# Where split weight chunks and MLP activations lie in SBUF: 224 bytes for stationary chunks, 32 bytes for the activations

## Chip, cores and metric

The kernel runs on one core of one Trainium2 chip. The metric is the device time of one execution in microseconds (us); lower is better. The time before is 747.07 us, the median of three runs.

## What is computed

A causal decoder trunk of two layers over 256 tokens of width 1024, in float32. Each layer is a mixer and a squared-ReLU MLP, with a LayerNorm after each:

```python
for layer in range(DEPTH):                      # DEPTH = 2
    h = rwkv_moba_mixer(x, ...) if layer % 2 == 0 else dilated_mixer(x, ...)
    x = layer_norm(ALPHA * x + h, ln1_g[layer], ln1_b[layer])
    mlp = square(relu(x @ w1[layer])) @ w2[layer]          # 1024 -> 4096 -> 1024
    x = layer_norm(ALPHA * x + mlp, ln2_g[layer], ln2_b[layer])
```

Layer 0's mixer is RWKV-7 time mixing (8 heads of 64) beside a block attention (4 heads of 128), with one input and one output projection. Layer 1's mixer is a dilated window attention: 8 heads of 128, each with one key, one value and three query projections.

## The kernel before

**Weights come as 211 chunks.** The host cuts every weight matrix into chunks of 128 partitions by 1024 floats (4096 bytes a partition, 512 KB each) in the order in which they are used. `Stream` (L51 on) loads them through SyncE's DMA queue into a ring of `raw` tiles. Chunks from number 17 on (`UNSPLIT`) are split: ScalarE copies `raw` to `hi` in the type float32r (L89), and VectorE, for twelve chunks GpSimd, writes the remainder `lo = raw - hi` (L91). `add_pairs` (L62) allocates the places for `hi` and `lo`: four pairs at the start, four more once layer 0's mixer has freed its memory. `place` (L93) hands them out in turn.

**A product is three float32r matmuls.** With both operands split, hi·hi, hi·lo and lo·hi are added in PSUM. Activations are split too: `xh`, `xl` (the layer's input, transposed), `yh`, `yl` (a mixer's output) and `hh`, `hl` (the MLP's hidden values). Each TensorE matmul has one operand that is loaded into the array beforehand, the *stationary* one (128 columns, so 512 bytes of each partition), and one that is *streamed* through it (256 or 512 columns, so 1024 or 2048 bytes of each partition). Every matmul here has its own weight load. There are two helpers:

- `wstat` (L207, matmuls at L218) keeps a weight chunk stationary and streams `xh` or `xl`, 256 tokens at a time. It is used for the projections into heads (L0's r, gate and block attention heads, all of layer 1's q and k) and for three quarters of the MLPs' first matrix. 90 chunks go this way after number 17, with 24 matmuls each: 2160.
- `xstat` (L221, matmuls at L223, L224, L225) keeps 128 tokens of an activation stationary and streams half a weight chunk, 512 columns. It is used for the output projections, value projections, the first quarter of the MLPs' first matrix (with `xh`, `xl` stationary) and the whole second matrix (`hh`, `hl` stationary). In the very last MLP, token half 1 has its right half in two streams of 256 columns (`acc_banks`, L295), so that 192 of its matmuls are 256 wide.

**Order of an MLP** (`mlp`, L354): a first quarter of the hidden values token by token (`by_token`, L338), then groups of eight `wstat` chunks (`up`) and of eight `xstat` chunks (`down`, 96 matmuls), and the last group in `tail` (L302), which ends each token half with its LayerNorm.

**Addresses.** A tile pool puts tiles one after another. The tile `x` (L1047), the LayerNorm tiles and, above them, the MLP tiles `r`, `s`, `hh`, `hl` lie in pools that are opened after the second four pairs. Nothing else about the layout is fixed by hand.

Of the kernel before, what the change touches and what calls it, by code (L numbers as in the profile page):

```python
# [11 lines left out]
F32 = mybir.dt.float32  # L12
F32R = mybir.dt.float32r
# [6 lines left out]
P = 128  # L20
T = 256
D = 1024
# [16 lines left out]

UNSPLIT = 17  # L40
ON_POOL = (34, 36, 37, 38, 39, 42, 100, 150, 151, 161, 164, 169)
NW1, NW2, NR, NR2 = 4, 4, 4, 2
NS4, NS2 = 13, 6
RIGHT = "right"
# [6 lines left out]
class Stream:  # L51
# [9 lines left out]

    def add_pairs(self, pool, n):  # L62

        new = [(pool.tile([P, D], F32R, name=f"hi{len(self.pairs) + i}"), pool.tile([P, D], F32R, name=f"lo{len(self.pairs) + i}"))
               for i in range(n)]
        self.pairs = new + self.pairs[self.pos:] + self.pairs[:self.pos]
        self.pos = 0
# [23 lines left out]
        eng.tensor_tensor(lo[:, cols], r[:, cols], hi[:, cols].bitcast(F32), ALU.subtract)  # L91

    def place(self, i):  # L93
        self.hl[i] = self.pairs[self.pos]
        self.pos = (self.pos + 1) % len(self.pairs)
        return self.hl[i]

# [22 lines left out]
def trunk(ctx: ExitStack, tc: tile.TileContext, w_all, x_nat, x_t, par_in, lora_in, gup2_in, ln_in,  # L120
# [80 lines left out]
    st.load(1 + NR)  # L201
    st.on_pool = set(ON_POOL)

# [32 lines left out]
    def bload(pool, i, nm):  # L236
        t = pool.tile([P, D], F32, tag=nm, name=f"{nm}{i}")
        nc.sync.dma_start(out=t, in_=ln_in[i:i + 1, :].partition_broadcast(P))
        return t
# [805 lines left out]
    cur["look"] = NW1 + NW2 - 2  # L1045
    lnp = ctx.enter_context(tc.tile_pool(name="lnp", bufs=1, reuse_waits="tile"))
    x = lnp.tile([P, 2, D], F32, name="x")  # L1047
    nc.sync.dma_start(out=x, in_=x_nat)
    g = bload(lnp, 0, "g")
    b = bload(lnp, 1, "b")  # L1050
# [258 lines left out]
```

## Time and profile before

| | |
|---|---|
| runs shown | 747.22, 743.59, 747.07 us (median 747.07) |
| the profiled execution | 743.96 us, its span 741.9 us |
| mean granted TensorE clock | 0.981 |
| PE (matmuls) busy | 711.9 us, 96% of the span |
| PEld (weight loads) busy | 632.2 us, 85% |
| DVE, ACT, POOL busy | 476.4, 333.9, 156.4 us |
| DMA | 122.61 MB, 165 GB/s in the mean |

PE is TensorE's matmuls and PEld its weight loads, which run beside matmuls; DVE is VectorE, ACT ScalarE, POOL GpSimd. Matmuls are pipelined: the duration that a row gives for one (0.28 or 0.39 us here) is longer than the distance from its start to the next one's start, and it is this distance, the *pace*, that a row of matmuls takes. Line numbers are those of the kernel before.

### The profile page before, as it was taken

How to read it: one execution, taken by the hardware profiler on the slowest of the kernel's cores; microseconds unless marked ns; L12 is line 12 of the kernel's file. 1: busy time of each engine (PE TensorE's matmuls, PEld its weight loads, DVE VectorE, ACT ScalarE, POOL GpSimd, SP SyncE). 2: the span in 40 equal slices, each digit the busy share in tenths (PEclk: the TensorE clock that was granted, in tenths of full speed). 3: DMA queues.
4: the chain of work that ended last, by engine and by line, in shares of the span. 5: the costliest groups of instructions: out<-in, count | busy, mean ns of one | idle time of the engine just before them, and what ended most of it. 6: DMA issues, size and time to landing. Idle time of an engine off the chain costs nothing. (4 is left out here: it accounts for less than half of the span.)

```text
span 741.9 us, 11557 instructions
## 1 busy us (share of the span) xinstructions
PE 711.9 (96%) x4572; PEld 632.2 (85%) x4572; DVE 476.4 (64%) x733; ACT 333.9 (45%) x485; POOL 156.4 (21%) x115
## 2 busy tenths in 40 slices
PE   9999998997999999999999899989999999999995
PEld 7867887986889889889879899988878898998985
DVE  3838973679686446546598668874497654464645
ACT  4712445253365335445255456545436453453420
POOL 3000041036100000000116767884131110000001
PEclk9999997998999999999999999999999999999998
DMA  8455461046584656555088433452537566555401
GB/s 305 142 176 181 137 190 44 30 175 252 169 284 151 200 188 197 173 199 180 20 297 302 143 114 115 149 168 83 169 125 245 168 198 189 190 192 172 142 1 58
DMA packets 40566, 122.61 MB, mean 165 GB/s; under 512 B 8128, under 2 KB 10816, under 8 KB 40384
## 3 DMA queue, kind: packets, MB, share of 16 engines
q1 hardware_dynamic: 37856, 119.94, 48.7%
q10 hardware_dynamic: 2656, 1.93, 0.9%
q8 instruction: 36, 0.59, 0.3%
q14 instruction: 18, 0.15, 0.1%
HBM read 119.49 MB, written 2.36 MB: 164 GB/s over the span
## 5 line engine op out<-in xcount | busy, mean ns | idle before, releaser
L91 DVE TENSOR_TENSOR lo<-raw,hi 128x1024 fp32r<-128x1024 f32 x182 | 236.4, 1303 | 145.4 <-ACT hi L89 143.7
L89 ACT CAST hi<-raw 128x1024 fp32r<-128x1024 f32 x194 | 202.1, 1048 | 207.1 <-PE bank L224 100.7
L218 PE MATMUL bank<-xh,hi 128*128 128x256 f32 x720 | 180.3, 288 | 0.0
L218 PE MATMUL bank<-xl,hi 128*128 128x256 f32 x720 | 178.2, 285 | 0.0
L218 PEld LDWEIGHTS bank<-xh,hi 128*128 128x128 f32 x720 | 138.8, 193 | 1.5 <-issue 0.7
L218 PEld LDWEIGHTS bank<-xl,hi 128*128 128x128 f32 x720 | 139.0, 193 | 0.5
L224 PE MATMUL bank<-hi,hl 128*128 128x512 f32 (+1 forms) x288 | 106.7, 371 | 1.9 <-DVE hl L234 1.9
L225 PE MATMUL bank<-lo,hh 128*128 128x512 f32 (+1 forms) x288 | 106.4, 370 | 0.0
L223 PE MATMUL bank<-hi,hh 128*128 128x512 f32 (+1 forms) x288 | 105.5, 370 | 0.3 <-ACT hh L233 0.3
L218 PE MATMUL bank<-xh,lo 128*128 128x256 f32 x720 | 101.8, 283 | 0.0
L218 PEld LDWEIGHTS bank<-xh,lo 128*128 128x128 f32 x720 | 93.0, 192 | 0.0
L266 POOL TENSOR_TENSOR rs<-rs,mhalf 128x1 f32<-128x1 f32 x8 | 7.7, 963 | 327.5 <-DVE rs L265 327.5
L854 POOL TENSOR_TENSOR qk<-qk,ropec 32x512 f32<-32x512 f32 x20 | 49.8, 2490 | 76.5 <-DVE sw L852 76.5
L224 PEld LDWEIGHTS bank<-hi,hl 128*128 128x128 f32 x288 | 54.0, 188 | 12.5 <-DVE hl L234 2.5
L223 PEld LDWEIGHTS bank<-hi,hh 128*128 128x128 f32 x288 | 53.9, 188 | 10.6 <-ACT hh L233 0.5
L225 PEld LDWEIGHTS bank<-lo,hh 128*128 128x128 f32 x288 | 54.0, 188 | 9.9
L210 PE MATMUL bank<-xst,raw 128*128 128x256 f32 x208 | 46.7, 384 | 0.5 <-DMA xst<-in_x_t_dram 0.5
L210 PEld LDWEIGHTS bank<-xst,raw 128*128 128x128 f32 x208 | 39.9, 193 | 7.4 <-DMA xst<-in_x_t_dram 1.2
L91 POOL TENSOR_TENSOR lo<-raw,hi 128x1024 fp32r<-128x1024 f32 x12 | 30.3, 2532 | 56.8 <-ACT hi L89 56.8
L225 PE MATMUL bank<-lo,xh 128*128 128x512 f32 x96 | 37.7, 393 | 0.6 <-DVE lo L91 0.6
L223 PE MATMUL bank<-hi,xh 128*128 128x512 f32 x96 | 38.0, 396 | 0.0
L224 PE MATMUL bank<-hi,xl 128*128 128x512 f32 x96 | 37.5, 391 | 0.1
(236 smaller groups left out, 896.0 us busy)
## 6 DMA issues: line engine op xcount, KB each, us to landing
raw<-in_w_all_dram SPq DMA_DIRECT2D x210, 512.0 KB, 3.5
g<-in_ln_dram SPq DMA_DIRECT2D x4, 512.0 KB, 5.1
b<-in_ln_dram SPq DMA_DIRECT2D x4, 512.0 KB, 6.7
dA<-abT ACTq DMA_DIRECT2D x2, 512.0 KB, 3.6
x<-in_x_nat_dram SPq DMA_DIRECT2D x1, 1024.0 KB, 4.9
dmask<-in_dmask_dram SPq DMA_DIRECT2D x1, 576.0 KB, 5.9
xst<-in_x_t_dram ACTq DMA_DIRECT2D x2, 256.0 KB, 5.6
xst<-in_x_t_dram SPq DMA_DIRECT2D x2, 256.0 KB, 5.7
```

What stands on the lines that cost most here:

```text
L89: self.nc.scalar.copy(hi[:, cols], r[:, cols])
L91: eng.tensor_tensor(lo[:, cols], r[:, cols], hi[:, cols].bitcast(F32), ALU.subtract)
L210: nc.tensor.matmul(ps, hl[:, k * P:(k + 1) * P], xraw(k), start=k == 0, stop=k == KT - 1)
L218: nc.tensor.matmul(ps, w[:, k * P:(k + 1) * P], a[:, k, :], start=n == 0, stop=n == 3 * KT - 1)
L223: nc.tensor.matmul(acc, ah, hi[:, cols], start=first, stop=False)
L224: nc.tensor.matmul(acc, al, hi[:, cols], start=False, stop=False)
L225: nc.tensor.matmul(acc, ah, lo[:, cols], start=False, stop=last)
L266: nc.gpsimd.tensor_tensor(rs, rs, mhalf, ALU.pow)
L854: nc.gpsimd.tensor_tensor(qk[0:32, :], qk[0:32, :], rc, MUL)
```

## The change

```diff
+STATIONARY = [1] * 9 + [0] * 4 + [1] * 14 + [0] * 8
+_MLP = [0] * 8 + [1] * 8 + [0] * 16 + ([1] * 8 + [0] * 8) * 2
+STATIONARY += _MLP + [0] * 4 + [1] * 32 + [0] * 12 + _MLP
+LINE, STAT_AT = 64, 56
@@ add_pairs
-        new = [(pool.tile([P, D], F32R, name=f"hi{len(self.pairs) + i}"), pool.tile([P, D], F32R, name=f"lo{len(self.pairs) + i}"))
+        new = [(pool.tile([P, D + LINE], F32R, name=f"hi{len(self.pairs) + i}"), pool.tile([P, D + LINE], F32R, name=f"lo{len(self.pairs) + i}"))
@@ place
-        self.hl[i] = self.pairs[self.pos]
+        o = STAT_AT if STATIONARY[i] else 0
+        self.hl[i] = tuple(t[:, o:o + D] for t in self.pairs[self.pos])
@@ trunk
     x = lnp.tile([P, 2, D], F32, name="x")
+    lnp.tile([P, 8], F32, name="pad")
```

`STATIONARY` tells of each chunk whether `wstat` will use it. A place for `hi` or `lo` becomes 1088 floats, 4352 bytes = 17 times 256. A chunk for `wstat` is written 56 floats, 224 bytes, into its place; a chunk for `xstat` at the place's beginning. An unused tile of 32 bytes behind `x` moves all that lies above it: the LayerNorm tiles, `vd`, and the MLP's `hh` and `hl`. The built program has the same instructions as before, in the same order and with the same waits, on every engine; only addresses differ. Of the operands of float32r matmuls they are, as the remainder of a tile's (or chunk's) first byte in the partition after division by 256:

| operand | before | after |
|---|---|---|
| `hi`, `lo` of a chunk that `wstat` keeps stationary | 128 | 96 |
| `hi`, `lo` of a chunk that `xstat` streams | 128 | 128 |
| `xh`, `xl`, `yh`, `yl` | 128 | 128 |
| `hh`, `hl` | 96 | 128 |

Slices inside these tiles start at multiples of 512 bytes, so that the remainders hold for them too. Call *distance* the stationary operand's remainder less the streamed one's. Before, it is 0 for `wstat`, 0 for `xstat` with `x` and `y`, and -32 for `xstat` with the MLP's `hh` and `hl`. After, it is -32 for `wstat` and 0 for every `xstat`. Of the other tiles, the LayerNorms' `g`, `b`, `u` go from 128 to 160.

## Rows read from the trace of the kernel before

**Rows 1.** The page: the span, and each engine's busy time, share and instructions.

```profile
span 741.9 us, 11557 instructions
...
PE 711.9 (96%) x4572; PEld 632.2 (85%) x4572; DVE 476.4 (64%) x733; ACT 333.9 (45%) x485; POOL 156.4 (21%) x115
```

**Rows 2.** The page: the chain that ended last, shares by engine, then by line.

```profile
PE 36%; DVE 6%; POOL 3%; issue 3%; ACT 1%; POOLq 0%; DVEq 0%
PE bank L218 17%; PE bank L225 6%; PE bank L224 6%; PE bank L223 5%; DVE lo L91 2%; POOL qk L854 2%; PE bank L1113 1%; POOL qk L856 1%; PE bank L1111 1%; DVE u L253 1%; ACT hi L89 1%; DVE sw L852 1%; DVE st L254 0%; ACT e L1119 0%; DVE x L279 0%
```

**Rows 3.** Groups by line and shape, PE: count, busy us, mean ns, idle before.

```profile
L218 PE MATMUL bank<-xh,hi 128*128 128x256 f32 x720 | 180.3, 288 | 0.0
L218 PE MATMUL bank<-xl,hi 128*128 128x256 f32 x720 | 178.2, 285 | 0.0
L218 PE MATMUL bank<-xh,lo 128*128 128x256 f32 x720 | 101.8, 283 | 0.0
...
L223 PE MATMUL bank<-hi,hh 128*128 128x512 f32 x224 | 87.9, 396 | 0.3 <-ACT hh L233 0.3
...
L223 PE MATMUL bank<-hi,hh 128*128 128x256 f32 x64 | 17.8, 280 | 0.0
```

**Rows 4.** Timeline in layer 1: a weight load starts with the matmul before its own.

```profile
300.83 0.19 PEld L218 LDWEIGHTS bank<-xh,hi 128*128 128x128 f32 x1
300.95 0.28 PE L218 MATMUL bank<-xh,hi 128*128 128x256 f32 x1
300.95 0.19 PEld L218 LDWEIGHTS bank<-xl,hi 128*128 128x128 f32 x1
```

**Rows 5.** The chain in order of time: start us, us, engine and line, count.

```profile
386.39 19.91 PE bank L218 x166
...
406.30 0.67 PE bank L1111 x6
...
583.39 17.27 PE bank L218 x144
```

**Rows 6.** Timeline, PE: first row of a `down` group and first row behind it.

```profile
303.83 0.39 PE L223 MATMUL bank<-hi,hh 128*128 128x512 f32 x1
...
326.23 0.28 PE L218 MATMUL bank<-xh,hi 128*128 128x256 f32 x1
```

**Rows 7.** Timeline, PE: first and last of a 512-wide run with `xh` stationary.

```profile
372.53 0.39 PE L223 MATMUL bank<-hi,xh 128*128 128x512 f32 x1
...
376.84 0.39 PE L224 MATMUL bank<-hi,xl 128*128 128x512 f32 x1
```

**Rows 8.** Timeline, PE: first and last of the 256-wide run at the end.

```profile
728.25 0.28 PE L223 MATMUL bank<-hi,hh 128*128 128x256 f32 x1
...
733.73 0.28 PE L225 MATMUL bank<-lo,hh 128*128 128x256 f32 x1
```

**Rows 9.** Two `up` groups by windows: PE, PEld, DVE, ACT, POOL busy; clock, DMA share, GB/s.

```profile
643.40:665.70 22.30, 22.30 (x188) 22.30 (x187) 13.69 (x14) 11.93 (x15) 0.00 (x0) 1.00 0.56 190
688.80:711.10 22.30, 22.30 (x189) 22.30 (x188) 13.69 (x14) 11.93 (x15) 0.00 (x0) 1.00 0.29 96
```

**Rows 10.** Waits of PE: us in total, times, longest.

```profile
PE bank L1111 <- POOL qk L856: 6.2, 4, 2.5
PE bank L290 <- DVE x L279: 5.6, 3, 3.5
...
PE bank L762 <- ACT W L753: 1.9, 1, 1.9
PE bank L750 <- DMA Tall<-dT: 1.7, 1, 1.7
```

**Rows 11.** Windows around one such wait in layer 1's heads, columns as in rows 9.

```profile
418.00:423.40 5.40, 2.91 (x25) 2.72 (x24) 3.60 (x5) 1.05 (x1) 5.32 (x3) 1.00 0.77 209
423.40:426.80 3.40, 3.40 (x13) 2.84 (x12) 1.85 (x7) 0.00 (x0) 1.82 (x2) 0.50 0.33 131
```

**Rows 12.** Groups by line and shape, DVE.

```profile
L91 DVE TENSOR_TENSOR lo<-raw,hi 128x1024 fp32r<-128x1024 f32 x182 | 236.4, 1303 | 145.4 <-ACT hi L89 143.7
...
L410 DVE TENSOR_TENSOR hl<-s,hh 128x512 fp32r<-128x512 f32 x24 | 16.6, 693 | 2.4
...
L848 DVE TENSOR_TENSOR yl<-ysq,yh 128x512 fp32r<-128x512 f32 x2 | 1.4, 693 | 1.4 <-ACT yh L847 1.4
```

## Prediction

> **What bounds the kernel now.** I read the page's busy times first: PE works 711.9 of 741.9 us, so all that PE's matmuls gain or lose shows, unless a wait swallows it [rows 1]. The chain that ended last agrees: its largest entries are the split products, L218 alone 17%, then L223 to L225 [rows 2]. The reader should see next how many there are: 3 x 720 = 2160 `wstat` matmuls; 3 x 224 = 672 `xstat` matmuls of 512 columns with the MLP's hidden values stationary; and 3 x 64 = 192 of 256 columns, all in the last MLP [rows 3]; of each of these two threes one row stands there.
>
> The durations in those rows overlap and don't add up. What counts is the pace, the distance from start to start. A weight load starts together with the matmul *before* its own: the load of `xl`'s product starts at 300.95, as the matmul of `xh`'s does [rows 4]. So while one operand streams, the next stationary one is read from the same memory, and the table of distances in the section on the change says how the two lie to each other. I measured the pace where nothing but one kind of matmul runs:
>
> - `wstat`, distance 0, 256 columns: 166 in 19.91 us is 119.9 ns; 144 in 17.27 us is 119.9 ns again [rows 5].
> - `xstat` with `hh`/`hl`, distance -32, 512 columns: one `down` group is 96 matmuls, 303.83 to 326.23, 233.3 ns [rows 6].
> - `xstat` with `xh`/`xl`, distance 0, 512 columns: 20 matmuls, 19 paces from 372.53 to 376.84, 226.8 ns [rows 7].
> - `xstat` with `hh`/`hl`, distance -32, 256 columns: 48 matmuls, 47 paces from 728.25 to 733.73, 116.6 ns [rows 8].
>
> The first two pairs of equal shape differ by distance: at 512 columns 0 is the better (226.8 against 233.3), at 256 columns -32 is (116.6 against 119.9). The change gives each shape the distance that was the better one, except the 192 narrow matmuls of the last MLP, which lose it.
>
> **The change part by part.**
>
> *Stationary chunks 224 bytes in.* 2160 `wstat` matmuls go from distance 0 to -32. The nearest row for 256 columns at -32 is rows 8, with other tiles and roles: there `hh` is stationary and a chunk streams. Taking its pace, each saves 119.9 - 116.6 = 3.3 ns: 2160 x 3.3 = 7.1 us. The bounds: at best a pace of 112 ns, which is the fastest that the chain shows for matmuls that each load 128 columns (L1111, six in 0.67 us [rows 5]), a gain of 2160 x 7.9 = 17.1 us. At worst -32 costs them what it costs 512 columns, 233.3 - 226.8 = 6.5 ns: a loss of 2160 x 6.5 = 14.0 us. I take rows 8, since they have the same width and distance.
>
> *MLP activations by 32 bytes.* 672 matmuls go from -32 to 0 and take the pace of rows 7: 672 x 6.5 = 4.4 us saved. The bounds are nothing (the pace belongs to the MLP's stretches, not to the distance) and this. 192 narrow ones go from 116.6 to `wstat`'s 119.9: 192 x 3.3 = 0.6 us lost.
>
> *Places of 4352 bytes.* 17 x 256 leaves each place at the same remainder, so the streamed chunks and everything that `xstat` does with `x` and `y` stay at 0. I cost it at nothing.
>
> *What the splits and LayerNorms do with moved tiles.* `hi` and `lo` of a stationary chunk now lie at 96 while `raw` stays at 128, and `g`, `b`, `u` at 160. VectorE's subtraction takes 693 ns both where its tiles are alike (L410, all at 96) and where they are not (L848, 224 and 128) [rows 12], so I cost it at nothing; VectorE's splits take 236.4 us in all and fit beside PE's work, and were each 2% longer that would hide there too.
>
> *What waits swallow.* A faster `wstat` helps only where PE doesn't then wait. In layer 1's heads PE waits for GpSimd's rotary four times, 6.2 us in all, once 2.5 us [rows 10], and after that one the granted clock is at 0.50, its lower level of 1.2 GHz, for 3.4 us [rows 11]. Some heads are thus paced by the chain through GpSimd, others by PE; 768 `wstat` matmuls (32 chunks of 24) lie there, a gain of 2.5 us, of which I strike half: 1.2 us. The 240 in layer 0's mixer stand between waits for a scratch transfer and for ScalarE (1.7 and 1.9 us, rows 10): of their 0.8 us I strike half, 0.4 us. The waits for the LayerNorms (L290, 5.6 us [rows 10]) come behind `xstat` and keep their length.
>
> The sum: 7.1 + 4.4 - 0.6 - 1.2 - 0.4 = 9.3 us. From the profiled execution's 743.96 that gives 734.7 us. This execution lies with the fastest run shown (743.59); the median, 747.07, is 3.1 us above it. I put the forecast between 734.7 and 737.8: **736.0 us**, some 1.3% faster.
>
> **A rule that speaks against it.** The trace has equal shapes at two paces, 226.8 and 233.3 ns, with the clock granted in full [rows 6, 7]. The Trainium skill, "TensorE: Matmul & The Clock Gate", section "Step-by-step: what each phase is for", says that TensorE has two independent read ports, and that "loading the next tile's weights doesn't steal SBUF read bandwidth from the running matmul"; by that rule the distance between the two operands is of no account, the sum is zero and the time stays at 744.0 us. The trace speaks against the rule as far as it goes: nothing in the instructions tells these two runs apart but the tiles that they read.
>
> The same page, section "Back-to-back issue gap", gives N / 2.4 + 2.5 ns for a warm matmul, an estimate of 109 ns at 256 columns and 216 ns at 512. The trace is above it at every distance, by 7 to 18 ns [rows 5 to 8], and by that page's figure alone no part of the sum changes.
>
> **The rivals.**
>
> *Address plays no part* (12%). The two paces would then come from what else runs in the MLP, writes by the splits or by DMA. For it: the two 512-wide paces never stand in one stretch. Against it: two `up` groups, one with a DMA share of 0.56 and one of 0.29, issue 188 and 189 matmuls in the same 22.30 us [rows 9], so traffic does not move the pace. Time: unchanged, 744 to 747 us.
>
> *Only the MLP's move works* (13%). The gain at 256 columns belongs to `xstat`'s roles or to its tiles, and `wstat` stays at 119.9. For it: no row shows `wstat` at any distance but 0. Against it: the weight loads and streams have the same widths as in rows 8. Time: 744.0 - 4.4 + 0.6 = 740.2 us, up to 743.3 beside the median.
>
> *Only the chunks' move works* (5%): 7.1 - 1.2 - 0.4 = 5.5 us gained, 0.6 us lost or not, so 738.5 to 739.1 us.
>
> *Stationary chunks at -32 are slower* (10%), the case on the other side. Place: each of the 2160 `wstat` matmuls. Price: the 6.5 ns that -32 costs 512 columns, 14.0 us, less the 3.8 us net of the activations: 744.0 + 10.2 = 754.2 us. It decides from a `wstat` pace of 119.9 + 3.8 / 2.16 = 121.7 ns up; slower by over 0.5% (3.7 us, about what a measurement of this kernel can tell from no change) needs 123.4 ns. For it: at 512 columns -32 is clearly the worse, and the narrow matmuls may be better there for another reason, as their two streams follow each other in one chunk. Against it: rows 8 are 256 columns at just this distance, below 119.9.
>
> **How the numbers follow.** The forecast has 60%: 733 to 739 us. Faster by over 0.5% than its base are nearly all of that, the case of the chunks alone and, with its 3.8 us on the border, half of the MLP's alone: 0.71. Within 0.5%: the other half, no effect of addresses and a little of the rest: 0.19. Slower by over 0.5%: 0.10. The range runs from 730, which is the sum without what waits swallow (10.9 us) on the fastest run and some 3 us of the way to the bound of 112 ns, to 747, no change on the slower runs; it leaves out the slow rival and the rest of the bound.
>
> **What would show it.** In the profile after: long runs of L218 in the chain at about 116.6 ns each (a `down` group aside, an `up` group of 192 in 22.4 us where it was 23.0); a `down` group of 96 in 21.8 us where it was 22.4; the last 48 matmuls at 119.9 ns; L1111's wait for GpSimd longer by a microsecond or so; L91 unchanged. An L218 pace of 119.9 proves the part on chunks wrong, one above 121.7 ns the sign. A `down` group still at 22.4 us proves that the distance is not what sets the pace. A second stretch at clock 0.50 in the heads would take back up to 1.7 us each (half of 3.4).

## The result and the profile after

The changed kernel took 734.24 us in the median of four runs (732.47 to 736.11), against 746.67 for the kernel before in the same rounds: a ratio of 0.985, 95% interval 0.982 to 0.988. Timed once more later, on another chip (run e7 below), it had 736.98 us against 746.33: 0.988, 0.984 to 0.993. The forecast was 736.0.

The profiled execution took 736.11 us, 7.9 us less than that of before. Lines of `wstat` and `xstat` are now L225 and L230 to L232. The page's first part:

```profile
span 734.0 us, 11556 instructions
...
PE 702.7 (96%) x4572; PEld 626.6 (85%) x4572; DVE 477.6 (65%) x733; ACT 333.8 (45%) x485; POOL 154.9 (21%) x115
```

PE has the same share of the span as before [rows 1] and the same 4572 matmuls: nothing was taken away, each takes less. One instruction fewer is in the span (11556 against 11557), a wait on SyncE's queue: in layer 0's mixer the first of two weight loads, issued at 160.66 us before and at 162.47 after, now waits for the release for which only the second waited. So one wait differs, other than the section on the change says. No gain comes from it: the stage that holds it, the first in the table below, got no shorter (211.4 us against 210.5). The chain that ended last, in order of time (start us, us, engine and line, count), has the long runs of stationary chunks:

```profile
578.00 16.81 PE bank L225 x144
636.98 22.41 PE bank L225 x192
681.61 22.41 PE bank L225 x192
```

All three are 116.7 ns a matmul; before it was 119.9 [rows 5]. The timeline of PE, the same three runs of `xstat` as in rows 6, 7 and 8:

```profile
302.34 0.40 PE L230 MATMUL bank<-hi,hh 128*128 128x512 f32 x1
...
324.13 0.28 PE L225 MATMUL bank<-xh,hi 128*128 128x256 f32 x1
...
369.35 0.39 PE L230 MATMUL bank<-hi,xh 128*128 128x512 f32 x1
...
373.65 0.39 PE L231 MATMUL bank<-hi,xl 128*128 128x512 f32 x1
...
720.19 0.28 PE L230 MATMUL bank<-hi,hh 128*128 128x256 f32 x1
...
725.82 0.28 PE L232 MATMUL bank<-lo,hh 128*128 128x256 f32 x1
```

A `down` group of 96 takes 21.79 us, 227.0 ns each (233.3 [rows 6]); the 19 paces with `xh` stationary 226.3 ns (226.8 [rows 7]); the last 47 paces 119.8 ns (116.6 [rows 8]). So every pace went where the distance between the two operands went, and the one that kept its distance stayed.

The same two `up` groups as in rows 9, by windows of the same length (PE, PEld, DVE, ACT, POOL busy, clock, DMA share, GB/s):

```profile
636.90:659.20 22.30, 22.30 (x193) 22.30 (x192) 13.68 (x14) 12.52 (x15) 0.00 (x0) 1.00 0.58 190
681.50:703.80 22.30, 22.30 (x193) 22.30 (x193) 13.69 (x14) 12.50 (x15) 0.00 (x0) 1.00 0.29 96
```

193 matmuls where 188 and 189 were, at the same clock, and again alike with much and with little DMA. PE's waits in layer 1's heads (us in total, times, longest):

```profile
PE bank L1119 <- POOL qk L863: 7.7, 4, 3.3
```

Windows around two of them, with columns as before:

```profile
414.00:421.00 7.00, 3.69 (x29) 3.42 (x29) 5.04 (x8) 1.71 (x3) 6.84 (x4) 1.00 0.78 240
421.00:424.40 3.40, 3.40 (x15) 3.13 (x14) 1.66 (x8) 0.37 (x1) 1.24 (x1) 0.50 0.14 53
494.00:500.00 6.00, 3.18 (x23) 2.84 (x22) 3.71 (x10) 0.17 (x1) 5.42 (x4) 1.00 0.61 208
```

The waits for GpSimd grew from 6.2 us [rows 10] to 7.7, as they would where a faster PE waits for the same rotary; the second trace of the change (e7) has 6.2 again. Of the stretches at the lower clock level (0.50) in the heads, of which the kernel before had two, at 423 us [rows 11] and at 502 us, one is still there.

Where the time went, by stage. The marks are starts of matmuls in the timeline: the first of an MLP's `wstat` groups, and the last `xstat` of MLP 0 with `hh`, `hl`; the last stage is from the last matmul to the span's end. us:

| | to MLP 0's `wstat` | MLP 0's rest | then to MLP 1's `wstat` (heads) | MLP 1's rest | end |
|---|---|---|---|---|---|
| before | 210.5 | 161.8 | 198.8 | 162.7 | 8.2 |
| after | 211.4 | 157.7 | 196.7 | 160.0 | 8.2 |
| e1, chunks alone | 211.4 | 160.0 | 197.8 | 160.8 | 8.2 |
| e2, activations alone | 214.0 | 159.6 | 198.9 | 161.9 | 8.2 |
| e7, the change again | 214.2 | 157.9 | 195.3 | 160.0 | 8.2 |
| e9, chunks at 76 bytes | 211.0 | 155.8 | 196.7 | 159.8 | 8.2 |

The two MLPs give 4.1 and 2.7 us, and 3.9 and 2.7 in the second profile of the change (e7); the heads give 2.1 and 3.5. The first column, layer 0's mixer, moves by up to 4 us between these runs, by 2.8 between the two of the change itself: PE waits there for a scratch transfer and for other engines, and stands at the lower clock for 17.1 us around 110 us in the run after, against 10.2 before. So the MLPs' columns tell more than the difference of two single profiles, 7.9 us here. Why the medians differ by 12.4 us in one set of rounds and by 9.3 in the other isn't shown, as the other executions were not traced.

### The profile page after: what moved, and what is told of

The parts are those of the page before. It is cut to its first block, busy times and chain, and to the rows that moved or that the text cites. A ratio compares the mean times of both kernels' runs of the same rounds, so it can differ in the third digit from the quotient of the medians.

```text
span 734.0 us, 11556 instructions
## 1 busy us (share of the span) xinstructions
PE 702.7 (96%) x4572; PEld 626.6 (85%) x4572; DVE 477.6 (65%) x733; ACT 333.8 (45%) x485; POOL 154.9 (21%) x115
## 5 line engine op out<-in xcount | busy, mean ns | idle before, releaser
L97 DVE TENSOR_TENSOR lo<-raw,hi 128x1024 fp32r<-128x1024 f32 x182 | 237.7, 1310 | 137.0 <-ACT hi L95 135.3
L225 PE MATMUL bank<-xh,hi 128*128 128x256 f32 x720 | 175.7, 284 | 0.0
L225 PE MATMUL bank<-xl,hi 128*128 128x256 f32 x720 | 173.8, 281 | 0.0
L225 PEld LDWEIGHTS bank<-xh,hi 128*128 128x128 f32 x720 | 136.2, 189 | 1.4 <-issue 0.7
L225 PEld LDWEIGHTS bank<-xl,hi 128*128 128x128 f32 x720 | 136.4, 189 | 0.5
L232 PE MATMUL bank<-lo,hh 128*128 128x512 f32 (+1 forms) x288 | 105.3, 366 | 0.0
L230 PE MATMUL bank<-hi,hh 128*128 128x512 f32 (+1 forms) x288 | 104.7, 367 | 0.3 <-ACT hh L240 0.3
L225 PE MATMUL bank<-xh,lo 128*128 128x256 f32 x720 | 100.3, 281 | 0.0
L225 PEld LDWEIGHTS bank<-xh,lo 128*128 128x128 f32 x720 | 91.5, 190 | 0.0
L230 PEld LDWEIGHTS bank<-hi,hh 128*128 128x128 f32 x288 | 54.2, 189 | 9.5 <-ACT hh L240 0.5
L232 PEld LDWEIGHTS bank<-lo,hh 128*128 128x128 f32 x288 | 54.2, 188 | 8.8
L232 PE MATMUL bank<-lo,xh 128*128 128x512 f32 x96 | 37.7, 393 | 0.6 <-DVE lo L97 0.5
L230 PE MATMUL bank<-hi,xh 128*128 128x512 f32 x96 | 38.1, 396 | 0.0
```

The source lines that it names most:

```text
L225: nc.tensor.matmul(ps, w[:, k * P:(k + 1) * P], a[:, k, :], start=n == 0, stop=n == 3 * KT - 1)
L230: nc.tensor.matmul(acc, ah, hi[:, cols], start=first, stop=False)
L232: nc.tensor.matmul(acc, ah, lo[:, cols], start=False, stop=last)
```

## The experiments

| run | edit | us, median | ratio to before, 95% interval |
|---|---|---|---|
| e1 | chunks alone | 740.25 (4 runs) | 0.992 (0.989 to 0.995) |
| e2 | activations alone | 744.58 (10) | 0.997 (0.994 to 1.000) |
| e3 | scan, 16-byte steps | 742.62 (1) | |
| e4 | `xh` moved instead | 742.47 (1) | |
| e5 | chunks at 64 bytes | 739.62 (6) | 0.993 (0.990 to 0.995) |
| e6 | scan, 4-byte steps | 740.01 (1) | |
| e7 | the change again | 736.98 (6) | 0.988 (0.984 to 0.993) |
| e8 | chunks at 52 bytes | 740.76 (6) | 0.993 (0.990 to 0.995) |
| e9 | chunks at 76 bytes | 733.10 (6) | 0.983 (0.981 to 0.986) |

My theory was that the pace of a matmul depends on the *distance*, the start of the next stationary operand less that of the streamed one, modulo 256 bytes. The rivals: the address of one operand alone, what else runs in a stretch, and that addresses don't matter.

**e1 and e2: the two parts alone.**

```diff
 e1, from the changed kernel
-    lnp.tile([P, 8], F32, name="pad")
 e2, from the changed kernel
-        o = STAT_AT if STATIONARY[i] else 0
+        o = 0
```

> Only the chunks' part of the change: places of 4352 bytes, stationary chunks 224 bytes in; the 32-byte tile is gone, so the MLP's hh and hl stay at remainder 96. By the distance theory (the pace of a matmul depends on the distance between the next stationary operand and the one that is streamed): wstat at 116.7 ns, xstat with hh/hl of 512 columns at 233.3, the last 48 narrow matmuls at 116.6; against the kernel before 2160 x 3.2 = 6.9 us less, of which up to 1.6 may be swallowed by waits: 5 to 7 us faster, some 0.7 to 0.9%. By the rival that the address of the activations' tiles alone matters: no change from before. By the rival that the two parts don't add: anything else, with the pair of runs e1 and e2 not summing to the change's 10 to 12 us.

> Only the activations' part: the 32-byte tile stays, every chunk lies at the beginning of its place of 4352 bytes. By the distance theory: wstat at 119.9 ns as before, xstat with hh/hl of 512 columns at 226.8, the last narrow ones at 119.8; against the kernel before 672 x 6.5 = 4.4 us less and 192 x 3.2 = 0.6 us more, 3.8 us faster, 0.5%. By the rival that the MLP's stretches are slow for what else runs in them: no change.

A row of the chain in order of time, an `up` group of MLP 1 in e1:

```profile
640.64 22.40 PE bank L225 x192
```

The same group in e2:

```profile
644.24 23.04 PE bank L225 x192
```

116.7 ns in e1, 120.0 in e2. A `down` group went the other way: 96 matmuls at 233.3 ns in e1, at 227.0 in e2 (starts of the first and the last 22.17 and 21.56 us apart). Both paces are as expected, and the MLPs add up: 1.8 and 2.2 us against the change's 4.1 in MLP 0, 1.9 and 0.8 against its 2.7 in MLP 1. In whole runs e1 is 6.0 us faster and e2 1.7 to 2.4, where 3.8 was expected; e2's interval just includes that. Together that is 7.6 to 8.4 us, short of the 10 to 12 that the expectation named and of the change's own 9.3 and 12.4. With intervals of 3.9 to 8.1 us for e1 and 0.2 to 4.5 for e2, whole runs can't tell whether the parts add; the stages do. e2 also leaves `wstat` at 120.0 ns with places of 4352 bytes, an odd multiple of 256, so that the wider places alone change nothing.

**e4: which address is it?** The kernel before with one line, and no change to the chunks' places:

```diff
+    const.tile([P, 8], F32, name="pad")
     xh = const.tile([P, KT, T], F32R, name="xh")
```

> The kernel before with one edit: an unused tile of 32 bytes ahead of xh moves everything allocated behind the first four pairs. xh, xl, yh, yl lie at remainder 160, pairs 0 to 3 at 128, pairs 4 to 7 at 160, hh and hl at 128. By the distance theory the pace alternates with the place: wstat 116.7 ns on pairs 0 to 3 (distance -32) and 119.9 on pairs 4 to 7 (0); xstat with hh/hl 226.8 on pairs 0 to 3 (0) and 233.3 on pairs 4 to 7 (-32). By the rival that the stationary operand's own address decides: wstat 119.9 on pairs 0 to 3 (stationary at 128, as before) and xstat with hh/hl 226.8 on all (stationary at 128). By the rival that the streamed operand's own address decides: wstat alike on all pairs.

The timeline of PE in MLP 0. The places are handed out in the order 7, 3, 0, 1, 2, 4, 5, 6. First `wstat`: the beginning of a chunk in pair 7, in pair 3 and in pair 0; then `xstat`: the beginning of pairs 0 and 1, and of pairs 4 and 5.

```profile
284.15 0.28 PE L219 MATMUL bank<-xh,hi 128*128 128x256 f32 x1
...
287.02 0.28 PE L219 MATMUL bank<-xh,hi 128*128 128x256 f32 x1
...
289.82 0.28 PE L219 MATMUL bank<-xh,hi 128*128 128x256 f32 x1
...
312.41 0.39 PE L224 MATMUL bank<-hi,hh 128*128 128x512 f32 x1
...
315.13 0.39 PE L224 MATMUL bank<-hi,hh 128*128 128x512 f32 x1
...
320.57 0.40 PE L224 MATMUL bank<-hi,hh 128*128 128x512 f32 x1
...
323.38 0.39 PE L224 MATMUL bank<-hi,hh 128*128 128x512 f32 x1
```

The chunk in pair 7 (distance 0) takes 2.87 us, 119.6 ns for each of its 24 matmuls; the next one, in pair 3 (-32), 2.80 us, 116.7 ns, with its stationary address at remainder 128, where before every chunk ran at 119.9. Twelve `xstat` matmuls take 2.72 us on pair 0 (distance 0) and 2.81 on pair 4 (-32), with `hh` at 128 both times. So neither the stationary nor the streamed address alone decides, and the stretch doesn't either: neighbours a few microseconds apart in one kernel differ as the theory says. The two single-address rivals and the rival of other traffic fall. The Trainium skill has it that loading the next weights costs the running matmul no read bandwidth ("TensorE: Matmul & The Clock Gate", "Step-by-step: what each phase is for"). The trace doesn't agree with what the prediction drew from that, a distance of no account: equal matmuls with equal loads take 119.6 or 116.7 ns by where their operands lie. Whether it is read bandwidth that is lost, no run here shows.

**e3: the cost at sixteen distances.** In the changed kernel the place of chunk `i` goes round in steps of 16 bytes:

```diff
-        o = STAT_AT if STATIONARY[i] else 0
+        o = 4 * (sum(s == STATIONARY[i] for s in STATIONARY[UNSPLIT:i]) % 16)
```

> A measurement of the disputed cost: chunk after chunk of either kind lies 0, 16, 32, ... 240 bytes into its place, counted round, so that each run of 24 wstat matmuls (or 12 xstat matmuls) has another distance, in steps of 16 bytes. By the distance theory: wstat at 119.9 ns where the offset is 0, 116.7 at 224, other values between 112 and 127 elsewhere, the same at the same offset in layer 0's MLP, in the heads and in the last MLP; xstat of 512 columns 226.8 at offset 0 and 233.3 at +32 (distance -32). By the rival that only two classes exist (64-byte lines, aligned alike or not): two values, alternating with 32 bytes. By the rival that addresses don't matter: one value, 119.9 and 226.8 to 233.3 by stretch.

Mean pace of `wstat` (ns, by chunk of 24 matmuls, five or six chunks each), worked out from the starts in the timeline:

| distance | 0 | 16 | 32 | 48 | 64 | 80 | 96 | 112 |
|---|---|---|---|---|---|---|---|---|
| ns | 119.6 | 118.7 | 118.3 | 118.7 | **113.6** | 118.8 | 117.8 | 119.9 |

| distance | 128 | 144 | 160 | 176 | 192 | 208 | 224 | 240 |
|---|---|---|---|---|---|---|---|---|
| ns | 119.5 | 119.1 | 119.9 | 118.1 | 116.0 | 116.7 | **116.7** | 118.8 |

At 0 and 224 they are the paces of the kernels before and after, in every part of the program. There are not two classes but many values. At 64 all six chunks are faster than the change's; one of them, from its first matmul to the next chunk's first, in the timeline:

```profile
288.32 0.28 PE L225 MATMUL bank<-xh,hi 128*128 128x256 f32 x1
...
291.05 0.28 PE L225 MATMUL bank<-xh,hi 128*128 128x256 f32 x1
```

2.73 us for 24 is 113.8 ns. At 192 three chunks had 117.7 to 118.0 and two 113.3, a first sign of what e5 shows. For `xstat` of 512 columns with `hh` the best distances were 0, 16 and 192 (229.8 to 230.4, with single chunks at 227.7), the worst 160 (234.0); 224 had 233.5.

**e5, e7: the best of the scan, and the change beside it.**

```diff
-LINE, STAT_AT = 64, 56
+LINE, STAT_AT = 64, 16
```

> The changed kernel with stationary chunks 64 bytes into their places in place of 224, all else alike: distance +64 for wstat. By the distance theory with the scan's values: wstat at 113.5 ns where the change has 116.7, all other paces as in the change; 2160 x 3.2 = 6.9 us less than the change, of which waits may swallow 1 to 2: some 0.7 to 0.9% faster than the change, some 17 us faster than before (ratio 0.976 to 0.979). By the rival that the scan's chunks at 64 were fast for their neighbours in the scan (each has another distance ahead of it and behind it): 116 to 120 ns and no gain over the change.

> The changed kernel itself, timed in the same rounds as e5 and the kernel before, to set e5 against it and to narrow its interval. By the sum of paces, 2160 x 3.2 + 672 x 6.5 - 192 x 3.2 = 10.7 us less than before, 735 to 737 us, a ratio of 0.985 to 0.987; a ratio under 0.984 would mean that waits or the clock have given something on top.

Here my theory failed in part. The chain of e5 in order of time:

```profile
386.60 19.55 PE bank L225 x166
...
581.57 16.33 PE bank L225 x144
640.08 22.61 PE bank L225 x192
684.93 22.61 PE bank L225 x192
```

The same kind of matmul at the same distance runs at 113.4 ns in one stretch (16.33 us for 144) and at 117.8 in the three others (22.61 for 192, 19.55 for 166), and keeps its pace through a whole stretch. So the distance alone doesn't set the pace: at 64 bytes there are two, and a long stretch stays with the one that it has when it begins. That fits the rival in the expectation, by which the scan's chunks at 64 owed their speed to what ran ahead of them; no run varied that alone. e5's ratio to before is 0.993, where the theory had 0.976 to 0.979, and e5 was slower than the change timed beside it (739.62 against 736.98 us); the two intervals overlap. The change's own ratio, 0.988, lies a little above what was expected, with 0.985 to 0.987 well inside its interval.

**e6: steps of four bytes**, to see whether lines of 16 or 64 bytes are at work.

```diff
-        o = STAT_AT if STATIONARY[i] else 0
+        n = sum(s == STATIONARY[i] for s in STATIONARY[UNSPLIT:i])
+        o = 12 + n % 9 if STATIONARY[i] else (0, 1, 2, 3, 4, 60, 61, 62, 63)[n % 9]
```

> A second scan, in steps of 4 bytes: wstat at distances 48, 52, ... 80 bytes, streamed chunks at places 0, 4, 8, 12, 16, 240, 244, 248, 252 bytes, so distances 0, -4, ... -16 and 16, 12, 8, 4 for xstat. If operands are read in lines of 16 bytes: the pace is the same for the four distances of one line, or changes at most at a boundary of 16. If every element counts: a smooth dip around 64 for wstat, and its bottom may lie off 64. By the rival that 64 bytes is a line: flat from 64 to 80, and the first step below 64.

| distance of `wstat` | 48 | 52 | 56 | 60 | 64 | 68 | 72 | 76 | 80 |
|---|---|---|---|---|---|---|---|---|---|
| ns, mean of 9 or 10 chunks | 120.5 | 114.5 | 117.9 | 119.7 | 114.1 | 118.4 | 118.3 | 114.3 | 118.8 |

A single float more or less changes the pace by up to 6 ns, and not at boundaries of 16 or of 64 bytes only; nor is it a smooth dip. All three expectations are missed. `xstat` of 512 columns is as sensitive: 228.5 ns at 0, 229.3 at -12, 236.3 at -4, 237.0 at 12. Some of the nine means for `wstat` hide two paces, as at 64 bytes in e5: at 48 single chunks had 118 or 123 ns, at 64 nine had about 114 and one 117.8.

**e8 and e9: two other distances with fast chunks**, `STAT_AT` 13 and 19 floats.

```diff
-LINE, STAT_AT = 64, 56
+LINE, STAT_AT = 64, 13
 e9
+LINE, STAT_AT = 64, 19
```

> The changed kernel with stationary chunks 52 bytes into their places, the distance at which all ten chunks of the second scan had 113.4 to 115.5 ns. If that pace holds in long runs: wstat at some 114 ns, the two MLPs' wstat groups (1248 matmuls outside the heads and layer 0's mixer) 3.4 us shorter than in the change, the heads little shorter since they then wait for GpSimd; 733 to 735 us, ratio to before 0.981 to 0.985. If two paces exist here too, as at 64 bytes, where a run keeps the one in which it begins: some stretches at 117 to 118 ns, and no gain over the change.

> The same with 76 bytes: seven of nine chunks of the second scan had 113.3 ns, one 114.5, one 120. If a chunk's pace is a matter of the distance: 113.3 ns throughout, the MLPs 4.2 us shorter than in the change, 732 to 734 us. If it has two paces: stretches at 113.3 and at 120, by what ran ahead of each, and a time between the change's less 4 us and the change's plus 4 us.

The chain of e8 in order of time:

```profile
388.98 16.10 PE bank L225 x134
...
586.08 16.33 PE bank L225 x144
644.59 21.81 PE bank L225 x192
688.63 21.81 PE bank L225 x192
```

The same view of e9:

```profile
381.07 15.22 PE bank L225 x134
...
635.73 21.77 PE bank L225 x192
679.74 21.77 PE bank L225 x192
```

At 52 bytes there are two paces again: 113.4 to 113.6 ns in most of MLP 1 (16.33 for 144, 21.81 for 192), 120.1 at the heads' beginning, and 120.0 all through MLP 0 (stretches of 192, from their starts). MLP 1's stretches of 192 begin at 115 to 120 and come to 113 within 14 matmuls, so that the pace can still change soon after the beginning. e8's 740.76 us miss the 733 to 735 of the one-pace case; as the case of two paces had it, there is no gain over the change. At 76 bytes both MLPs run at 113.4 (21.77 for 192); only some single chunks between the heads' scores have 120. e9 is the fastest kernel of the study: 733.10 us, 13.0 us under before. Against the change (e7), e9 has 2.1 us less in MLP 0 and 0.2 in MLP 1, where 4.2 in all were expected. That figure, like e8's 3.4, counts 1248 `wstat` matmuls in the MLPs; they have 48 chunks of 24, 1152, so 1152 x 3.4 ns = 3.9 us were due. The rest, some 1.6 us, went to a stretch of 3.4 us at the lower clock level in MLP 1 (from 574.1 us on): the last few `xstat` matmuls and transposes ahead of a `wstat` stretch took 2.56 us in it, 1.36 in the trace of the change, and the `wstat` stretch's beginning some 0.4 us more. That e9 beats the kernel before is shown; whether it beats the change isn't settled, with 0.983 against the change's 0.985 and 0.988 and intervals that overlap.

## Why the prediction was right, point by point

- **Stationary chunks 224 bytes in**: right in size and sign. 116.7 ns was measured, 116.6 taken from rows 8. 2160 x 3.2 us/1000 is 6.9 us; e1 alone had 6.0.
- **MLP activations by 32 bytes**: right in sign, a little large. In steady groups 227.0 ns, as taken; but the mean over all 512-wide matmuls with `hh` and `hl` stationary that follow one another without a wait fell from 233.2 to 227.9, 5.3 and not 6.5 ns, so that the term is 3.6 us and not 4.4. The 192 narrow ones went to 119.8 as forecast.
- **Places of 4352 bytes cost nothing**: right, 226.3 ns with `xh` stationary, and `wstat` at 120.0 in e2.
- **Moved tiles on VectorE cost nothing**: the mean split went from 1303 to 1310 ns, 0.5%, and it hides. The page after has it:

```profile
L97 DVE TENSOR_TENSOR lo<-raw,hi 128x1024 fp32r<-128x1024 f32 x182 | 237.7, 1310 | 137.0 <-ACT hi L95 135.3
```

- **What waits swallow**: struck at 1.6 us, and by the traces true in kind: the wait for GpSimd is 6.2 us with `wstat` at 119.9 ns (before and e2), 7.5, 7.7 and 6.2 at 116.7 (e1, the change, e7), and 8.4 to 8.7 at the faster distances (e5, e8, e9). The size can't be told. And the count of stretches at the lower clock in the heads, two before and one after, moves as much time (1.7 us each) the other way. I had not reckoned with a gain there; rows 11 show one of the two.
- **The total**: the measured paces give 6.9 + 3.6 - 0.6 = 9.9 us before any wait, against the 9.3 of the sum; e7 has 9.3. The first rounds have 12.4, 2.5 more than the paces account for. That part is likely luck: the four executions behind it had granted clocks of 0.977 to 0.986, e7's six 0.969 to 0.982.
- **The rivals**: that only one part works, or none, is excluded by e1, e2 and e4. The slow one needed a `wstat` pace over 121.7 ns; at -32 no chunk that ran without a gap had one, though single chunks at another distance did (123 ns at 48 in e6).
- **The theory**: what the prediction had too simple is the theory under it. It read two distances and two widths as better and worse; that a distance can have two paces, and that single floats count, no row of before showed. At -32 and 0, the two that the change uses, one pace was seen in every long stretch of every run.

## What to carry to other kernels

Where matmuls with a weight load each follow one another without a gap, measure the pace (start to start) of equal ones in different stretches: if it differs, compare where the next stationary and the streamed operand lie, before looking for another cause. An offset within each place makes this cheap to scan in one run, but take the winner only after a run with that offset throughout, since a short chunk in a scan can show a pace that a long stretch doesn't keep.

## What the runs showed of the hardware

- The pace of a float32r matmul of 256 columns with its own load ran from 113.4 to 120 ns in long stretches, with nothing changed but the operands' start addresses; for 512 columns from 226.3 to 233.3, and to 237 in the scan of single floats.
- At 0 and -32 it goes by the difference of the two addresses: moved together they leave it as it is (e4). Neither 16 nor 64 bytes is its grain; a step of 4 bytes, from 72 to 76, took it from 118.3 to 114.3 ns.
- A pace like 116.7 ns is a mean. The starts in the trace, read to the nanosecond, are 120 ns apart almost throughout at distance 0 (before), but 113, 116, 117 or 118, and 120 in turn at -32 (the change), and 113, 113 and 114 in turn at 76 (e9).
- At 52 and 64 bytes a stretch has one of two paces and keeps it for up to 192 matmuls: 113.4 or 120.0, and 113.4 or 117.8 ns. At 76 bytes only single chunks had the slower one. What decides at the beginning was not tried, nor why a distance has the pace that it has. Both stay open.
